# Score tiles and groups of transposes in pairs in the attention heads of an encoder trunk

## The chip, the cores and the metric

The kernel runs on one core of a Trainium2 chip. The core has a matrix engine (TensorE, PE in the profile; its weight loads have a row of their own, PEld), three engines for elementwise work (VectorE or DVE, ScalarE or ACT, GpSimd or POOL), and DMA queues, most of them issued from SyncE (SP). PE reads its operands from on-chip memory and writes into PSUM, from where ACT and DVE fetch the results. The metric is the device time of one execution in microseconds. Three runs of the kernel before gave 1676.1, 1676.44 and 1677.04; the median is 1676.44.

## The reference

Two sequences of 512 tokens and 1024 features go through a trunk of two layers: a Fourier mixing layer and an attention layer, each followed by an MLP with a squared ReLU. Only the attention matters here. It has 8 query heads of 128 features that share 2 key and value heads; queries and keys are normalised and rotated first.

```python
def one_block(q_blk):
    s = jnp.einsum("bqkgd,bskd->bkgqs", q_blk, k)
    p = jax.nn.softmax(s, axis=-1)
    return jnp.einsum("bkgqs,bskd->bqkgd", p.astype(v.dtype), v)
```

So for each of 2 x 8 pairs of sequence and head, a 512 x 512 matrix of scores is made from queries and keys, each row becomes a softmax, and the result weighs the values.

## The kernel before

Operands of matmuls are split into a high and a low half of a reduced 32-bit format, and a product of two split operands is made of three matmuls (high by high, high by low, low by high) that accumulate in one PSUM tile: `mm3`, lines L81 to L83. A split is a cast on ACT (L86) and a subtraction on DVE (L87). Elsewhere in the kernel the same product is written as `product` (L927). PSUM holds eight tiles of 128 x 512.

The work on one head has these parts:

- `transpose_q` (L1497): four 128 x 128 transposes turn the query of a head into one PSUM tile, which is split.
- `scores` (L1508 to L1512), once for each of four tiles of 128 queries: three matmuls; the row maximum, negated, on DVE (L1508); the exponential with the row's sum on ACT (L1510); the reciprocal of the sum on DVE (L1511); the normalisation on POOL (L1512). Each tile of probabilities takes one of eight buffers of a pool of temporaries.
- `transpose_p` (L1518), once for each of four tiles of 128 keys: four transposes, one out of each of the head's four probability tiles, fill one PSUM tile, which is split. So the first group already needs all four tiles of the head.
- `values`: twelve matmuls over the four transposed tiles; the result is copied out of PSUM on ACT (L1534), and for the first sequence it is split too.

The loop over the heads is staggered: in turn n it makes the scores of head n and transposes the probabilities of head n - 1, then the query of head n + 1 is transposed, then the values of head n - 1 are multiplied. Turns 1 to 15 have both scores and transposes; the last turn, 16, has transposes and values only. The scores of the first head stand before the loop.

```python
for n in range(1, len(heads) + 1):
    pts, nxt = [], []
    for t in range(NT):
        if n < len(heads):
            nxt.append(scores(*heads[n], qT, t))
        k, both = transpose_p(probs, t)
        pts.append(k)
        ...
    if n + 1 < len(heads):
        qT = transpose_q(*heads[n + 1])
    values(*heads[n - 1], pts)
```

Two further jobs are threaded through the loop. From the third turn, a piece of deferred normalisation and rotation of queries (`todo`, on ACT, DVE and POOL) follows the first group of transposes. From the seventh turn, weights of the output projection are loaded ahead over SP, and in each of eight turns one of them is split (`fresh`; L86 and L87 with the operand w); that split is placed behind the split of the turn's last transposed tile and behind the last exponential and reciprocal.

What sets the order: in blocks marked `manual_schedule` the engines named there keep the written order. The loop over heads stands in no such block, so a planner orders every engine's instructions by its own estimates, with the written order as preference. The projection behind the loop (from L1740) again has PE's order written out.

Of the kernel before, what the change touches and what calls it, by code (L numbers as in the profile page):

```python
# [44 lines left out]
def trunk_kernel(ctx, tc, x_in, xt_in, y_out, tables, rope, gfour, gcol, grow, gfin,  # L45
# [22 lines left out]
    def tm(shape=(P, 512), dt=F32):  # L68
        return tmp.tile(list(shape), dt, tag="t2", name=nm("t"))

    def small(n=4):
        return sm.tile([P, n], F32, tag="s", name=nm("s"), padded_shape=[P, 8])

    def ps():
        return psp.tile([P, 512], F32, tag="ps", name=nm("ps"))
# [4 lines left out]
    def mm3(out, lh, ll, rh, rl, first, last):  # L80
        nc.tensor.matmul(out, lh, rh, start=first, stop=False)  # L81
        nc.tensor.matmul(out, lh, rl, start=False, stop=False)  # L82
        nc.tensor.matmul(out, ll, rh, start=False, stop=last)  # L83
# [5 lines left out]
    def behind(x, y, sync=False):  # L89

        kind = mybir.DependencyClass.Sync if sync else mybir.DependencyClass.NoSync
        tc.add_manual_dep(x.ins, y.ins.name, mybir.DependencyInfo(kind, mybir.DependencyReason.SCHED_ONLY),
                          reason="order")
# [1338 lines left out]
    def head_squares(raw, h0, n, ss, scale=1.0):  # L1432
        junk = tm((P, n * HD), BF16)
        for h in range(h0, h0 + n):
            nc.scalar.activation(junk[:, (h - h0) * HD : (h - h0 + 1) * HD], raw[:, h * HD : (h + 1) * HD],
                                 AF.Square, scale=scale, accum_out=ss[:, h : h + 1])
# [56 lines left out]
    def transpose_q(q, h):  # L1493
        pt = ps()
        c = (h % 2) * HD
        for t in range(NT):
            nc.tensor.transpose(pt[:, t * P : (t + 1) * P], qr[q, h // 2][:, t, c : c + HD], ident)  # L1497
        qT = slot([P, 2, 512], F32R)
        split(qT[:, 0], qT[:, 1], pt)
        return qT  # L1500

    def scores(q, h, qT, t):
        kk = kT[q, h // 4]
        s = ps()
        cols = slice(t * P, (t + 1) * P)
        mm3(s, qT[:, 0, cols], qT[:, 1, cols], kk[:, 0], kk[:, 1], True, True)
        m, sm_ = small(1), small(1)
        nc.vector.tensor_reduce(m[:, :1], s, AX.X, ALU.max, negate=True)  # L1508
        p = tm()
        last_made[:] = [nc.scalar.activation(p, s, AF.Exp, bias=m[:, :1], accum_out=sm_[:, :1]),  # L1510
                        nc.vector.reciprocal(sm_[:, :1], sm_[:, :1])]  # L1511
        nc.gpsimd.tensor_scalar(p, p, sm_[:, :1], 1.0, ALU.mult, ALU.mult)  # L1512
        return p

    def transpose_p(probs, sc):
        pt = ps()
        for t in range(NT):
            nc.tensor.transpose(pt[:, t * P : (t + 1) * P], probs[t][:, sc * P : (sc + 1) * P], ident)  # L1518
        k = slot([P, 2, 512], F32R)
        return k, split(k[:, 0], k[:, 1], pt)  # L1520

    def values(q, h, pts):
        o = ps()
        c = (h // 4) * HD
        for sc in range(NT):
            vh, vl = vt[q][0][:, sc, c : c + HD], vt[q][1][:, sc, c : c + HD]
            mm3(o, vh, vl, pts[sc][:, 0], pts[sc][:, 1], sc == 0, sc == NT - 1)
        i, j = h // 2, h % 2
        name = "b11" if h < 4 else "b21"
        if j == 0:  # L1530
            heads_out.f[q, i] = slot([P, 2, 512], F32)
            if q == 0:
                heads_out.b.setdefault(name, []).append([slot([P, 2, 512], F32R) for _ in range(2)])
        nc.scalar.copy(heads_out.f[q, i][:, j], o)  # L1534
        if q == 0:
            hi, lo = heads_out.b[name][-1]
            split(hi[:, j], lo[:, j], o)
# [143 lines left out]
    heads = [(q, h) for q in range(NSEQ) for h in range(NH)]  # L1681
    raw, ss = slot([P, 1024], F32), small(8)
    with tc.manual_schedule(engines={ET.Activation}):
# [4 lines left out]
        qT = transpose_q(*heads[1])  # L1688
# [9 lines left out]
    for n in range(1, len(heads) + 1):  # L1698
        pts, nxt = [], []
        for t in range(NT):  # L1700
            if n < len(heads):
                nxt.append(scores(*heads[n], qT, t))
            k, both = transpose_p(probs, t)
            pts.append(k)
            if t == NT - 1 and fresh:
                for a, b, c in zip(fresh.pop(), both, last_made):
                    behind(a, b)
                    if nxt:
                        behind(a, c)
            if n > 2 and t == 0:  # L1710
                for _ in range(3 if n == 3 else 1):
                    next(todo, None)
        last = nxt[-1] if nxt else last
# [3 lines that stand above are left out]
        if n == 2:  # L1717
            head_squares(raw, 4, 4, ss)
        probs = nxt
        if n > 6:  # L1720
            next(first_rows, None)
# [373 lines left out]
```

## Time and profile before

The profiled execution took 1677.68 us, of which the span from the first to the last instruction is 1675.9 us.

| | |
|---|---|
| median of three runs | 1676.44 us |
| profiled execution; its span | 1677.68 us; 1675.9 us |
| PE busy | 1662.2 us (99%) |
| PEld, DVE, ACT, POOL busy | 1386.9, 1265.2, 870.0, 391.0 us |
| mean granted clock of PE | 0.999 |
| loop over heads, first transposes to the projection | 844.56 to 965.65 us |

How to read it: the busy time of an engine is a share of the whole span and says nothing of a single stage. The row of a stretch gives the same numbers for that stretch alone. The chain of work that ended last is followed back from the last instruction; a millisecond of PE in it means that PE waited for nothing in that time. A row of the timeline gives start, length, engine, line, operation, output and inputs, and in brackets the idle time before it with what ended it. Rows of consecutive instructions of one kind are merged (x4), and as matmuls are pipelined their lengths overlap: the distance between starts is what one of them costs.

### The profile page before, as it was taken

To read this page: it belongs to the slowest core of one execution; us is meant where nothing else is said; L and a number is where in the kernel's file an instruction comes from. 1 tells how busy PE (TensorE), PEld (TensorE's weight loads), DVE (VectorE), ACT (ScalarE), POOL (GpSimd) and SP (SyncE) were. 2 spreads that over 40 slices of the span, in tenths; PEclk is the share of its full clock that TensorE was granted. 3 is DMA by queue.
4 is the path that set the end of the run, shared out by engine and by line. 5 is a ranking of instruction groups with operands and counts; after the bars stand their busy time and mean duration, and the time that the engine had idled before them with its cause. 6 is when DMAs were issued, how large, how long until landed. Compare 5 with 4: busy or idle time off the path is not lost.

```text
span 1675.9 us, 22279 instructions
## 1 busy us (share of the span) xinstructions
PE 1662.2 (99%) x7845; PEld 1386.9 (83%) x7845; DVE 1265.2 (75%) x1847; ACT 870.0 (52%) x1536; POOL 391.0 (23%) x364
## 2 busy tenths in 40 slices
PE   9999999999999999999999999999999999999998
PEld 8988888888888888888888888888888888888887
DVE  8779786557886869869888877777855487978865
ACT  6766444446343435446688854554454552433334
POOL 3321443221000001324454302004422220000002
PEclk9999999999999999999999999999999999999999
DMA  9843655449775757525501155334544696757522
GB/s 309 255 160 107 210 182 188 156 163 371 257 226 164 246 172 236 177 69 191 172 1 39 63 178 212 126 119 168 210 145 166 219 381 191 230 157 246 168 101 101
DMA packets 122048, 303.00 MB, mean 181 GB/s; under 512 B 12200, under 2 KB 13352, under 8 KB 121936
## 3 DMA queue, kind: packets, MB, share of 16 engines
q1 hardware_dynamic: 98576, 254.05, 43.6%
q0 software_dynamic: 8960, 21.05, 5.9%
q10 hardware_dynamic: 14400, 26.48, 4.2%
q8 instruction: 61, 1.00, 0.2%
q14 instruction: 51, 0.42, 0.1%
HBM read 218.11 MB, written 82.38 MB: 179 GB/s over the span
## 4 chain that ended last, share of the span: by engine, by line
PE 95%; DVE 2%; DMA 1%; ACT 1%; issue 1%; POOL 0%; SPq 0%; DVEq 0%; POOLq 0%; ACTq 0%
PE ps L927 73%; PE ps L83 6%; PE ps L81 6%; PE ps L82 6%; PE ps L1518 2%; DMA u<-x 0%; DMA u<-w_four 0%; PE ps L1497 0%; DVE w L87 0%; PE ps L191 0%; DMA raw<-w_up 0%; PE ps L496 0%; PE ps L493 0%; DVE u L238 0%; DVE raw L975 0%
## 5 line engine op out<-in xcount | busy, mean ns | idle before, releaser
L927 PE MATMUL ps<-u,w 128*128 128x512 f32 x4944 | 1131.1, 389 | 1.3 <-DVE u L1730 1.3
L927 PEld LDWEIGHTS ps<-u,w 128*128 128x128 f32 x4944 | 926.5, 188 | 196.3 <-ACT u L958 1.9
L86 ACT CAST w<-raw 128x1024 fp32r<-128x1024 f32 (+1 forms) x216 | 213.8, 994 | 311.8 <-PE ps L927 233.8
L87 DVE TENSOR_TENSOR w<-raw,w 128x1024 fp32r<-128x1024 f32 (+1 forms) x216 | 252.4, 1172 | 76.3 <-ACT w L86 76.1
L86 ACT CAST u<-u 128x1024 fp32r<-128x1024 f32 x144 | 145.0, 1047 | 84.1 <-PE ps L927 38.3
L87 DVE TENSOR_TENSOR u<-u,u 128x1024 fp32r<-128x1024 f32 x144 | 173.8, 1233 | 17.0 <-ACT u L86 15.7
L927 PE MATMUL ps<-u,u 128*128 128x512 f32 x600 | 143.1, 389 | 0.5 <-DVE t L1012 0.5
L1133 DVE TENSOR_TENSOR u<-ps,u 128x512 f32<-128x512 f32 x160 | 109.4, 685 | 39.2 <-PE ps L927 37.0
L1160 POOL DMA_DIRECT2D raw<-w_sum x32 | 27.7, 865 | 469.3 <-DMA raw<-w_sum 195.6
L1043 POOL TENSOR_TENSOR u<-u 128x512 f32<-128x512 f32 x28 | 37.6, 1344 | 426.0 <-ACT u L940 426.0
L927 PEld LDWEIGHTS ps<-u,u 128*128 128x128 f32 x600 | 112.4, 188 | 24.5 <-DVE t L1012 0.9
L81 PE MATMUL ps<-u,u 128*128 128x512 f32 (+2 forms) x340 | 128.7, 380 | 0.0
L83 PE MATMUL ps<-u,u 128*128 128x512 f32 (+2 forms) x340 | 124.0, 366 | 0.0
L82 PE MATMUL ps<-u,u 128*128 128x512 f32 (+2 forms) x340 | 123.6, 365 | 0.0
L182 POOL TENSOR_TENSOR t<-t,t 128x512 f32<-128x512 f32 (+1 forms) x54 | 77.6, 1442 | 186.7 <-ACT t L178 185.8
L939 ACT ACTIVATE t<-t 128x512 f32<-128x512 f32 x64 | 40.5, 632 | 110.0 <-DVE t L1012 96.5
L83 PEld LDWEIGHTS ps<-u,u 128*128 128x128 f32 x340 | 64.2, 189 | 10.8 <-DVE u L87 0.3
L87 DVE TENSOR_TENSOR u<-ps,u 128x512 fp32r<-128x512 f32 (+3 forms) x112 | 68.1, 634 | 5.6 <-ACT u L86 5.1
L82 PEld LDWEIGHTS ps<-u,u 128*128 128x128 f32 x340 | 64.4, 189 | 8.4 <-DVE u L87 0.3
L81 PEld LDWEIGHTS ps<-u,u 128*128 128x128 f32 x340 | 64.4, 189 | 7.8
L999 DVE TENSOR_TENSOR t<-ps,u 128x512 f32<-128x512 f32 x32 | 22.0, 687 | 59.7 <-PE ps L927 56.0
L86 ACT CAST u<-ps 128x512 fp32r<-128x512 f32 (+3 forms) x112 | 59.4, 556 | 7.6 <-PE ps L1518 6.1
(265 smaller groups left out, 2015.3 us busy)
## 6 DMA issues: line engine op xcount, KB each, us to landing
raw<-w_up SPq DMA_DIRECT2D x80, 512.0 KB, 4.6
u<-spill_t SPq DMA_DIRECT2D x60, 512.0 KB, 6.9
raw<-w_sum SPq DMA_DIRECT2D x56, 512.0 KB, 5.6
u<-spill_b SPq DMA_DIRECT2D x45, 512.0 KB, 6.4
spill_t<-u SPq DMA_DIRECT2D x84, 256.0 KB, 2.0
spill_b<-t ACTq DMA_DIRECT2D x60, 256.0 KB, 4.3
raw<-w_row SPq DMA_DIRECT2D x28, 512.0 KB, 5.1
park<-u SPq DMA_DIRECT2D x24, 512.0 KB, 4.5
```

The lines of the kernel that those rows point to most:

```text
L81: nc.tensor.matmul(out, lh, rh, start=first, stop=False)
L82: nc.tensor.matmul(out, lh, rl, start=False, stop=False)
L83: nc.tensor.matmul(out, ll, rh, start=False, stop=last)
L86: hi = nc.scalar.copy(dst_hi, src)
L87: return hi, eng.tensor_sub(dst_lo, src, f32(dst_hi))
L182: nc.gpsimd.tensor_add(acc[q][:, :n], acc[q][:, :n], s[:, :n])
L927: nc.tensor.matmul(o, w[x][:, sl], h[k][y], start=first and k + i == 0, stop=k == n - 1 and i == 2, skip_group_check=not first)
L939: nc.scalar.activation(t, src, AF.Relu)
L1043: eng.tensor_sub(t[:, 0], b12, b11)
L1133: return nc.vector.tensor_add(x, o, x)
L1160: nc.gpsimd.dma_start(s[:, 1], w[:, 3], accum_op=ALU.add)
L1518: nc.tensor.transpose(pt[:, t * P : (t + 1) * P], probs[t][:, sc * P : (sc + 1) * P], ident)
```

## The change

Two score tiles are made in one go, at the even tiles, where one was made at each tile. The groups of transposes stay where they are in the loop, so that two score tiles are followed by two groups of transposes, twice per head. No instruction is added or taken away, and no operand changes.

```diff
     for n in range(1, len(heads) + 1):
         pts, nxt = [], []
         for t in range(NT):
-            if n < len(heads):
-                nxt.append(scores(*heads[n], qT, t))
+            if n < len(heads) and t % 2 == 0:
+                nxt += [scores(*heads[n], qT, i) for i in range(t, t + 2)]
             k, both = transpose_p(probs, t)
             pts.append(k)
             if t == NT - 1 and fresh:
```

## The prediction

> **What bounds the kernel now.** I read the page first: busy time by engine, then the chain that ended last.
>
> ```profile
> span 1675.9 us, 22279 instructions
> ...
> PE 1662.2 (99%) x7845; PEld 1386.9 (83%) x7845; DVE 1265.2 (75%) x1847; ACT 870.0 (52%) x1536; POOL 391.0 (23%) x364
> ...
> PE 95%; DVE 2%; DMA 1%; ACT 1%; issue 1%; POOL 0%; SPq 0%; DVEq 0%; POOLq 0%; ACTq 0%
> ```
>
> TensorE (PE) is busy for all but 13.7 us of the span and carries 95% of the chain. So I narrow the views to the loop over heads, which is all that the change touches. The table by stretch gives it one row, and the waits of that stretch name who held up PE's weight loads (PEld), which run just ahead of its matmuls.
>
> ```profile
> 844.56:965.65 121.09, 120.84 (x683) 100.45 (x682) 106.65 (x227) 105.12 (x258) 49.07 (x70) 1.00 0.11 36
> ```
>
> ```profile
> PEld ps L1518 <- POOL t L1512: 1.3, 4, 0.6
> PEld ps L82 <- DVE u L87: 0.3, 2, 0.2
> PEld ps L83 <- DVE u L87: 0.3, 1, 0.3
> ```
>
> The columns of the first are length, then busy time of PE, PEld, DVE, ACT and POOL, granted clock, DMA share, GB/s. The stage is 121.09 us long, 7.2% of the span; PE is busy for 120.84 of them at full clock, while VectorE (DVE, 106.65) and ScalarE (ACT, 105.12) follow close. The only waits of weight loads come to 1.9 us, and 1.3 of them are for the probabilities that POOL normalises (L1512) and the transposes (L1518) read. A reordering on PE can win here what is lost to waits or to switching between kinds of work; it can lose whatever it makes late on DVE and ACT.
>
> **The change, part by part.** It adds and removes no instruction. In each of 15 heads (n = 1 to 15) the order s0 T0 s1 T1 s2 T2 s3 T3 becomes s0 s1 T0 T1 s2 s3 T2 T3 (s: a score tile of three matmuls, L81 to L83; T: a group of four transposes, L1518). So 30 times a score tile moves ahead of one group of transposes, and its maximum (DVE), exponential (ACT), reciprocal (DVE) and normalisation (POOL) move with it ahead of that group's cast (ACT) and subtraction (DVE). Behind T3 stand, as before, the transposes of the next query (Q, L1497) and the twelve matmuls of the values. No DMA moves against another; the deferred rotary step that follows the first T of a head (n > 2) now stands behind two score tiles.
>
> Switching on PE. The chain in order of time, from the fourth head on, prices each kind in both neighbourhoods:
>
> ```profile
> 861.11 0.23 PE ps L83
> 861.35 0.44 PE ps L1518 x4
> 861.78 0.23 PE ps L81
> ...
> 863.39 0.23 PE ps L83
> 863.62 0.44 PE ps L1518 x4
> 864.06 0.44 PE ps L1497 x4
> 864.49 0.23 PE ps L81
> ```
>
> A group of four transposes between matmuls takes 0.44 us (861.35 to 861.78), and so does each of two groups in a row (863.62 to 864.49 is 0.87); a matmul takes 0.23 us before and behind a group. So merging groups saves 0.87 to 0.88 against 0.87: between 0 and 0.01 us per merge, 2 merges per head, 15 heads, 0 to 0.3 us. A coarser reading gives a wider upper end, from the starts of one undisturbed head (timeline of PE):
>
> ```profile
> 946.18 0.60 PE L1518 MATMUL ps<-ident,t 128*128 128x128 f32 x4
> ...
> 949.60 0.60 PE L1518 MATMUL ps<-ident,t 128*128 128x128 f32 x4
> ...
> 950.39 0.48 PE L81 MATMUL ps<-u,u 128*128 128x512 f32 x1
> 950.70 0.40 PE L82 MATMUL ps<-u,u 128*128 128x512 f32 x1
> ...
> 952.79 0.39 PE L82 MATMUL ps<-u,u 128*128 128x512 f32 x1
> ...
> 953.47 0.39 PE L82 MATMUL ps<-u,u 128*128 128x512 f32 x1
> ...
> 953.93 0.60 PE L1518 MATMUL ps<-ident,t 128*128 128x128 f32 x4
> 960.55 2.21 PE L1518 MATMUL ps<-ident,t 128*128 128x128 f32 x16
> 962.52 0.47 PE L81 MATMUL ps<-u,u 128*128 128x512 f32 x1
> ```
>
> From 950.70 to 953.93 are 14 matmuls: 0.231 each. Three turns of s and T take 3.42 (946.18 to 949.60), so a lone group is 1.14 - 0.692 = 0.448; the eight transposes with the matmul behind them take 1.10 (949.60 to 950.70), so two groups together are 0.869. That is 0.027 per merge, 0.8 us in all. I take 0.2, nearest to the chain, whose rows are ends and not starts; the ends are 0 and 0.8.
>
> Waits that go. The undisturbed head lasts 953.93 - 946.18 = 7.75 us. Heads with rotary work in them last longer:
>
> ```profile
> 860.05 0.60 PE L1518 MATMUL ps<-ident,t 128*128 128x128 f32 x4
> ...
> 868.09 0.38 PE L1518 MATMUL ps<-ident,t 128*128 128x128 f32 x2
> ...
> 876.10 0.49 PE L1518 MATMUL ps<-ident,t 128*128 128x128 f32 x3
> ...
> 907.51 0.60 PE L1518 MATMUL ps<-ident,t 128*128 128x128 f32 x4
> ```
>
> 860.05 to 876.10 is two heads, 16.05 against 15.50: 0.55 lost. 876.10 to 907.51 is four heads, 31.41 against 31.00: 0.41 lost. The last sixteen transposes take 1.97 us (960.55 to 962.52) against 16 x 0.11 = 1.76: 0.2 lost. All that can be won back is 1.2 us. What these wait for is close to late even in the undisturbed head (POOL's and DVE's timeline; the fourth probability tile is the one on POOL):
>
> ```profile
> 952.89 0.70 POOL L1512 TENSOR_SCALAR t<-t,s 128x512 f32<-128x512 f32 x1 [0.56 <-DVE s L1511]
> ```
>
> ```profile
> 950.11 0.69 DVE L87 TENSOR_TENSOR u<-ps,u 128x512 fp32r<-128x512 f32 x1
> 950.72 0.68 DVE L1508 TENSOR_REDUCE s<-ps 128x1 f32<-128x512 f32 x1
> 951.32 0.15 DVE L1511 RECIPROCAL s<-s 128x1 f32<-128x1 f32 x1
> 951.39 1.27 DVE L87 TENSOR_TENSOR u<-ps,u 128x512 fp32r<-128x512 f32 x2
> 952.57 0.15 DVE L1511 RECIPROCAL s<-s 128x1 f32<-128x1 f32 x1
> 953.04 1.08 DVE L87 TENSOR_TENSOR w<-u,w 128x512 fp32r<-128x512 f32 x1 [0.32 <-ACT w L86]
> ```
>
> The tile is ready at 953.59 and first read at 953.93: 0.34 us to spare. After the change two score tiles instead of one lie between the values and T0, which makes T0 3 x 0.23 = 0.69 us later, and s3 ends one group, 0.44 us, earlier. So up to 1.1 us is added to those 0.34, and waits for POOL should mostly go. Since the same engines serve a burst now, I book half of the 1.2: 0.6 us; ends 0 and 1.2.
>
> What is late next. DVE spaces maxima and subtractions by 0.60 (950.72 to 951.32) and reciprocals by 0.07. From the end of s2 to the second matmul of the next head's s0, which reads the low half of Q, PE will need s3 0.69, T2, T3 and Q 1.31, values 2.77 and one matmul 0.23: 5.0 us. In it DVE has two maxima, three subtractions and two reciprocals, 3.14 us, and the subtraction of T1 if that is left over, 0.60: 1.2 us to spare. Before, Q's subtraction ended at 951.39 + 1.27 = 952.66 and was read at 953.47, 0.8 to spare; T3's low half, done by about 952.05, was read at 952.79, 0.7 to spare. So the cover is not thinner than now, unless DVE takes the split of a kept weight (L87, w<-u,w, 1.08 us, one in each of eight heads) in between. I book 0.2 us for stray waits of that sort; ends 0 and the slow rival's price below. PSUM: a head takes ten of the pool's tiles, eight stand in the pool, so a buffer comes round after eight tenths of 7.75, 6.2 us. The fourth score tile, begun three matmuls before 949.60, so at 948.9, is held until its exponential, which ends before the reciprocal at 952.57: 3.7 us; a burst that puts two more places of 0.60 in front of it still leaves 1.3 us. I book nothing; without that cover it would be the same 0.60 per head as the slow rival's.
>
> The sum, on the profiled execution (1677.68 us, of which 1675.9 is span): 1677.68 - 0.2 - 0.6 + 0.2 = 1677.1. That execution lies 1.24 above the median of the runs, 1676.44, so against the median the forecast is 1675.8. Its own range is 1674.4 (0.8 + 1.2 won) to 1676.8 (nothing won, 0.4 of strays).
>
> **The rivals.** No change at all (0.12): no block with a written order stands around the loop, so the planner may fall back to single turns where it thinks a tile not ready; the same page of waits would remain and the time would be 1676.4. For it: at 868.09 it already split a group of transposes. Against: the plain head follows the written order exactly.
>
> Switching costs more than I read (0.08). Behind a group the first matmul occupies 950.39 to 950.70, 0.31 instead of 0.23. If the 0.08 were lost time and not the end of the last transpose, 30 merges would give 2.4, and with all waits gone 1676.44 - 2.4 - 1.2 = 1672.8, 0.2% faster. Against it speaks the chain, where the matmul behind a group takes 0.23.
>
> Slower (0.18): the burst of s2, s3, T2, T3, Q makes DVE late in the eight heads with a weight split. The split is due behind T3's subtraction and the fourth reciprocal; now it stands behind Q's subtraction too (953.04 comes last). If in the burst it slips ahead of Q's subtraction, 1.2 us to spare becomes 0.1, and ACT's share of the chain, a cast and an exponential, is not yet in that. If it costs one DVE place, 0.60, in eight heads, the loss is 4.8 less the 0.6 of waits won: 1676.44 + 4.2 = 1680.6. It decides from about 0.5 us per head in eight heads (4.0 less 0.6 is 3.4). Against it: PE can take T0 or s1 of the next head meanwhile, as the planner's own swaps show, and DVE has 14.4 us of idle time in the stage.
>
> The clock falls (0.01). The longest run of transposes grows from eight to twelve, 1.3 us. If those ran at half clock, 12 x 0.11 x 15 = 20 us would be added: 1696. Against it: sixteen transposes ran within 960.55 to 962.52, and the stage's granted clock reads 1.00. The Trainium skill ("TensorE: Matmul & The Clock Gate", Part 4: PE-mode transpose) says that transposes do not count as activity for the clock as matmuls do, which speaks for this rival; by that rule longer runs of transposes could let the clock fall, and the trace shows no such fall even in a longer run.
>
> The stage behind moves (0.03): a loop that ends earlier or later changes what the transfers for the next stage collide with; nothing here prices that, and I put it at 2 us to either side, since PE's order there is written out.
>
> **How the numbers follow.** Forecast 0.58, the others as given. About 0.2%, 3.4 us, is what a measurement of this kernel can tell from no change: faster means below 1673.1, slower above 1679.8. Faster: half of the switching rival, 0.04. Slower: somewhat over half of the slow rival, 0.10, and the clock, 0.01: 0.11. The rest, 0.85, is the same. The range 1673.0 to 1680.0 takes in the forecast, no change, the mild half of the switching rival and the mild part of the slow one; it leaves out about 0.04 + 0.08 + 0.01.
>
> **What would show it.** Right: PE's timeline shows six matmuls, then eight transposes, then six matmuls, then twelve transposes; two groups in a row take 0.87; the undisturbed head stays within 0.06 of 7.75; the waits of L1518 for L1512 fall below 1.3; 876.10 to 907.51's counterpart shortens towards 31.0. Wrong: waits of L82 or L83 for L87 grow beyond 1 us, above all in the later heads; the head falls below 7.65; or the time moves outside the stage.

## The result, and the profile after

The kernel with pairs takes 1679.55 us (median of 19 runs) against 1676.52 for the kernel before (19 runs): the ratio is 1.0017, 95% interval 1.0011 to 1.0024, so 3.0 us slower. Forecast was 1675.8, 0.6 us faster. The time lies within the range that was given, but on the wrong side of the kernel before.

The page of the kernel with pairs:

```profile
span 1678.0 us, 22288 instructions
...
PE 1664.5 (99%) x7845; PEld 1387.3 (83%) x7845; DVE 1267.0 (76%) x1847; ACT 870.0 (52%) x1536; POOL 392.2 (23%) x364
...
PE 92%; DVE 4%; ACT 1%; DMA 1%; issue 1%; POOL 0%; SPq 0%; DVEq 0%; ACTq 0%; POOLq 0%
```

PE is still busy 99% of the span, but its share of the chain has fallen from 95% to 92% and that of DVE has risen from 2% to 4%. The loss lies in the loop over heads alone. To measure that stage in both traces I take the first matmul on a weight of the last projection before the loop (PE's timeline) and the first copy behind it (L1750, whose row gives first and last start), and for what follows the first transpose of the output (L1864). First the kernel before, then the one with pairs; in each, one row of the timeline and two rows of the views by line:

```profile
838.29 0.49 PE L81 MATMUL ps<-w,u 128*128 128x512 f32 x1
```

```profile
L1750 ACT COPY t<-ps x4: 582/589/589, 968.4 to 982.0; 128x512 f32<-128x512 f32 x4
```

```profile
L1864 PE MATMUL ps<-ident,u x16: 270/272/273, 1641.0 to 1642.7; 128*128 128x128 f32 x16
```

```profile
837.29 0.49 PE L81 MATMUL ps<-w,u 128*128 128x512 f32 x1
```

```profile
L1750 ACT COPY t<-ps x4: 589/589/589, 970.9 to 984.5; 128x512 f32<-128x512 f32 x4
```

```profile
L1864 PE MATMUL ps<-ident,u x16: 270/272/273, 1643.5 to 1645.2; 128*128 128x128 f32 x16
```

The stage takes 968.4 - 838.3 = 130.1 us before and 970.9 - 837.3 = 133.6 with pairs, 3.5 more. From there to the output it is 672.6 in both. So nothing came from the stages behind. The span grew by only 2.1 us, because the profile with pairs reaches the stage 1.0 us earlier and is 0.4 us shorter behind the first transpose of the output.

The waits of weight loads from 844.5 to 970 us, with pairs:

```profile
PEld ps L82 <- DVE u L87: 5.1, 15, 0.6
PEld ps L81 <- ACT u L86: 1.5, 5, 0.4
PEld ps L83 <- DVE u L87: 1.4, 2, 0.7
PEld ps L1518 <- POOL t L1512: 0.4, 1, 0.4
```

The waits for POOL's probabilities fell from 1.3 to 0.4 us, as forecast. In their place stand 8.0 us of waits for splits (L86, L87), where there were 0.6; not all of it is lost time, since a weight load runs ahead of its matmul. Of the 5.1 us in the first row, 3.8 lie between 863 and 902 us, in stretches 3 to 7 of the table below; the second products of the values (L82), which read the low halves of the transposed tiles, wait there. The 1.4 us of L83 are two waits for the low half of a query, both behind 916 us.

Where this falls is seen turn by turn. The table gives the time from one start of a query's transposes (L1497 in PE's timeline) to the next, so "3" is the stretch from Q in turn 3 to Q in turn 4. Stretches 4 to 7 hold one group of the deferred rotary products each, stretch 3 the first steps of that work; weight splits fall into the stretches from 9 on. The clear stretches are 2 and 8, and 9, where the split stands behind Q's subtraction before and after (914.54 and 914.82 in DVE's timelines) and costs 0.02 us at most.

| kernel | 1, 2 | 3 | 4 to 7 (rotary) | 8, 9 | 10 to 13 (weight splits) | 1 to 13 |
|---|---|---|---|---|---|---|
| before | 7.76 7.72 | 8.32 | 7.76 7.90 7.87 7.89 | 7.72 7.74 | 7.74 7.73 7.74 7.73 | 101.6 |
| pairs | 7.74 7.71 | 8.48 | 8.17 8.14 8.17 8.11 | 7.71 7.71 | 8.46 7.89 8.02 8.53 | 104.8 |

Clear stretches (2, 8, 9) became shorter by 0.01 to 0.03. The rotary stretches lost 0.22 to 0.41 each, 1.2 us in all; stretches 10 to 13 lost 2.0 us; stretch 3 lost 0.16. Two different things happen there.

*Weight splits.* DVE's timeline of stretch 10 with pairs, then POOL's, then PE's:

```profile
920.44 1.29 DVE L87 TENSOR_TENSOR u<-ps,u 128x512 fp32r<-128x512 f32 x2
921.64 0.15 DVE L1511 RECIPROCAL s<-s 128x1 f32<-128x1 f32 x1
922.12 1.08 DVE L87 TENSOR_TENSOR w<-u,w 128x512 fp32r<-128x512 f32 x1 [0.32 <-ACT w L86]
923.12 0.68 DVE L87 TENSOR_TENSOR u<-ps,u 128x512 fp32r<-128x512 f32 x1
```

```profile
921.96 0.70 POOL L1512 TENSOR_SCALAR t<-t,s 128x512 f32<-128x512 f32 x1 [0.72 <-DVE s L1511]
```

```profile
922.96 0.39 PE L82 MATMUL ps<-u,u 128*128 128x512 f32 x1
923.19 0.40 PE L81 MATMUL ps<-u,u 128*128 128x512 f32 x1
923.85 0.50 PE L83 MATMUL ps<-u,u 128*128 128x512 f32 x1 [0.27 <-DVE u L87]
```

The weight's subtraction now runs ahead of the subtraction that makes Q's low half (923.12); in the rows of before it came last, behind Q's. PE has begun two score tiles of the next head and stops, since the third product needs that half. On ACT the weight's cast runs ahead of Q's as well:

```profile
921.45 0.64 ACT L86 CAST w<-u 128x512 fp32r<-128x512 f32 x1
921.96 0.61 ACT L86 CAST u<-ps 128x512 fp32r<-128x512 f32 x1
```

The split stands ahead of Q's subtraction in stretches 10, 11 and 13. In 10 and 13 POOL's normalisation began first, the split takes 1.08 us, and these stretches lose 0.72 and 0.80; in 11 DVE began first, the split takes 0.69 (930.52), and the loss is 0.16. In stretch 12 it stands behind Q's subtraction (939.14), and there the planner chose another order of casts and subtractions for the turn, which loses 0.28.

*Rotary products.* One such step, two products on DVE (L1474) and one on POOL (L1471); before, then with pairs:

```profile
869.67 0.48 DVE L1474 TENSOR_TENSOR t<-u,u 128x128 f32<-128x128 f32 x2
```

```profile
869.01 0.74 POOL L1471 TENSOR_TENSOR t<-u,u 128x256 f32<-128x256 f32 x1
```

```profile
870.42 1.02 DVE L1474 TENSOR_TENSOR t<-u,u 128x128 f32<-128x128 f32 x2
871.37 0.68 DVE L87 TENSOR_TENSOR u<-ps,u 128x512 fp32r<-128x512 f32 x1
```

```profile
870.53 0.77 POOL L1471 TENSOR_TENSOR t<-u,u 128x256 f32<-128x256 f32 x1
```

Before, POOL had all but finished when DVE began. With pairs both begin within 0.11 us, and DVE's two products take 1.02 us in place of 0.48. The subtractions of the transposed tiles stand behind them, and the values wait for what these make: with pairs, in each of the four stretches, one second product of the values (L82) starts 0.46 us behind the first and the third 0.34 behind that, where 0.23 is usual.

### The profile page after: what moved, and what is told of

Same layout as the page of the kernel before. It is cut to its first block, busy times and chain, and to the rows that moved or that the text cites. A ratio compares the mean times of both kernels' runs of the same rounds, so it can differ in the third digit from the quotient of the medians.

```text
span 1678.0 us, 22288 instructions
## 1 busy us (share of the span) xinstructions
PE 1664.5 (99%) x7845; PEld 1387.3 (83%) x7845; DVE 1267.0 (76%) x1847; ACT 870.0 (52%) x1536; POOL 392.2 (23%) x364
## 4 chain that ended last, share of the span: by engine, by line
PE 92%; DVE 4%; ACT 1%; DMA 1%; issue 1%; POOL 0%; SPq 0%; DVEq 0%; ACTq 0%; POOLq 0%
PE ps L927 73%; PE ps L83 5%; PE ps L82 5%; PE ps L81 5%; PE ps L1518 1%; DVE u L87 1%; DVE s L1508 1%; DMA u<-x 0%; DVE w L87 0%; DMA u<-w_four 0%; ACT t L1510 0%; PE ps L191 0%; PE ps L496 0%; DMA raw<-w_up 0%; PE ps L493 0%
## 5 line engine op out<-in xcount | busy, mean ns | idle before, releaser
L86 ACT CAST w<-raw 128x1024 fp32r<-128x1024 f32 (+1 forms) x216 | 213.6, 994 | 310.5 <-PE ps L927 243.9
L87 DVE TENSOR_TENSOR w<-raw,w 128x1024 fp32r<-128x1024 f32 (+1 forms) x216 | 252.5, 1172 | 75.8 <-ACT w L86 75.6
L86 ACT CAST u<-u 128x1024 fp32r<-128x1024 f32 x144 | 145.1, 1047 | 81.4 <-PE ps L927 36.8
L87 DVE TENSOR_TENSOR u<-u,u 128x1024 fp32r<-128x1024 f32 x144 | 173.4, 1231 | 17.5 <-ACT u L86 16.4
L81 PE MATMUL ps<-u,u 128*128 128x512 f32 (+2 forms) x340 | 126.5, 375 | 0.0
L82 PE MATMUL ps<-u,u 128*128 128x512 f32 (+2 forms) x340 | 125.0, 368 | 0.4
L83 PE MATMUL ps<-u,u 128*128 128x512 f32 (+2 forms) x340 | 124.0, 366 | 0.5 <-DVE u L87 0.5
L82 PEld LDWEIGHTS ps<-u,u 128*128 128x128 f32 x340 | 64.3, 189 | 13.6 <-DVE u L87 5.1
L83 PEld LDWEIGHTS ps<-u,u 128*128 128x128 f32 x340 | 64.1, 189 | 11.4 <-DVE u L87 1.4
L81 PEld LDWEIGHTS ps<-u,u 128*128 128x128 f32 x340 | 64.2, 189 | 10.3 <-ACT u L86 1.5
L87 DVE TENSOR_TENSOR u<-ps,u 128x512 fp32r<-128x512 f32 (+3 forms) x112 | 68.4, 634 | 5.4 <-ACT u L86 4.7
L1512 POOL TENSOR_SCALAR t<-t,s 128x512 f32<-128x512 f32 x64 | 47.2, 738 | 74.9 <-DVE s L1511 49.7
```

The costliest lines, as they stand in the source:

```text
L86: hi = nc.scalar.copy(dst_hi, src)
L87: return hi, eng.tensor_sub(dst_lo, src, f32(dst_hi))
```

## The experiments

Theory W: the weight split ahead of Q's subtraction is one part of the loss. Theory R: the rotary products that run beside POOL's are the other. Theory B, the rival: the burst as such, two score tiles and two groups, makes DVE late in any turn.

Each kernel below was run 11 times (the last 5 times) beside the kernel before. The intervals are some 0.09%, 1.4 us, to either side, so the whole time of a kernel can hardly tell a single loss from none. The stretches can: the pairs alone and the second kernel below have the same order on every engine, and in the stretches that its edit does not touch their profiles agree within 0.03 us. The expectations of the first two kernels count turns from one first group of transposes to the next, so their numbers differ a little from the stretches here.

**The weight split behind Q.** The weight's cast and subtraction are put behind Q's as an order told to the planner; nothing else is edited.

```diff
-        split(qT[:, 0], qT[:, 1], pt)
+        q_made[:] = split(qT[:, 0], qT[:, 1], pt)
...
-                for a, b, c in zip(fresh.pop(), both, last_made):
+                for a, b, c in zip((weight := fresh.pop()), both, last_made):
...
             qT = transpose_q(*heads[n + 1])
+            [behind(a, b) for a, b in zip(weight, q_made)]
```

> Pairs kept; in the turns with a weight split, that split is put behind Q's cast and subtraction. In the profile of the pairs it ran ahead of Q's subtraction in some turns, at 922.12 and at 946.55 for 1.08 us each, and these two turns lasted 8.48 and 8.54 against 7.71. Theory W (the weight split delays the query of the next head): the turns from 916.17 to 956.98 come back to about 7.71, which gives back up to 2.3 us of their excess; the time falls from 1679.6 to 1677.3 to 1678. Theory R (the rotary step on DVE and POOL is the cause): the two long turns may shrink, but the time falls by less than 0.7, since the loss lies in the turns before. Theory B (the burst of two score tiles and two groups makes DVE late in every turn): no change beyond 0.5 us.

It takes 1678.2 us against 1676.8 of the kernel before in the same set, ratio 1.0008 (1.0000 to 1.0017): 1.4 us above it, where the pairs alone are 3.0 above. Stretches 10 to 12 are 7.71, 7.76 and 7.73; the rotary stretches stay at 8.13 to 8.18. Stretch 13 stays at 8.08: at 944.25 a product of the values starts 0.45 us behind the one before it. With the next edit added it is 7.72, although the order on every engine is the same in both kernels, so what is left there is not a matter of order; its cause stays open. Q's subtraction and the weight's, in that order, in DVE's timeline of this kernel:

```profile
945.15 0.69 DVE L87 TENSOR_TENSOR u<-ps,u 128x512 fp32r<-128x512 f32 x1 [0.28 <-ACT u L86]
945.76 0.68 DVE L87 TENSOR_TENSOR w<-u,w 128x512 fp32r<-128x512 f32 x1
```

In the stretches this is W, and not B. The planner's other orders change along with it: the products of two score tiles that were interleaved on PE in stretches 10, 11 and 13 stand in plain order again, and so do the casts and subtractions of turn 12.

**The rotary products apart.** POOL's product is told to wait for DVE's two.

```diff
-            eng.tensor_mul(t1, x, every(table[:, 0, t]))
+            first = eng.tensor_mul(t1, x, every(table[:, 0, t])) if eng is nc.vector else None
             ...
-                nc.vector.tensor_mul(t2[:, :, sl], x[:, :, other], every(table[:, 1, t, sl]))
+                made = nc.vector.tensor_mul(t2[:, :, sl], x[:, :, other], every(table[:, 1, t, sl]))
+            first or behind(eng.tensor_mul(t1, x, every(table[:, 0, t])), made, True)
```

> Pairs kept; POOL's product of the rotary step waits until DVE's two products of that step are done, so that the two engines no longer read and write on-chip memory for it at the same time. Order on every engine unchanged. In the profile of the pairs the two DVE products took 1.02 to 1.11 us where POOL's ran beside them, before 0.47 to 0.48. Theory R: the products fall back to about 0.5, the four turns from 868.16 to 900.76, which last 8.11 to 8.18, come to about 7.75, and the time falls by 1.3 to 1.8, to about 1678. Theory W: these turns get no shorter than by 0.1 each and the time stays at 1679.6. Theory B: no change either.

1678.18 us, ratio 1.0005 (0.9996 to 1.0014): again 1.4 above the kernel before. The rotary stretches fall to 7.71, 7.72, 7.75 and 7.73, while 10 to 13 keep 8.47, 7.86, 8.04 and 8.53. DVE's products (now L1473) and POOL's (now L1474):

```profile
870.37 0.48 DVE L1473 TENSOR_TENSOR t<-u,u 128x128 f32<-128x128 f32 x2
```

```profile
871.02 0.73 POOL L1474 TENSOR_TENSOR t<-u,u 128x256 f32<-128x256 f32 x1 [0.53 <-PE ps L1518]
```

All four engines run the same instructions in the same order as with pairs alone; only POOL's product starts later. So the 0.5 to 0.7 us that DVE lost per step, and the 0.4 us that each of these stretches won back, are the price of running side by side, and R holds.

**Both edits, with pairs and with single turns.** The same two edits, once on the pairs and once on the kernel before.

> Pairs kept, with both edits: the weight split behind Q's subtraction, and POOL's rotary product behind DVE's. Theories W and R together: the gains add, 1679.6 - 2.0 - 1.5 = about 1676, level with the kernel before or up to 0.8 us faster, since merged groups of transposes cost a little less. Theory B: 1679 or more.

> Single score tiles and groups as in the kernel before, with the same two edits as in the run with both. It tells whether pairs win or lose once both covers are restored. If pairs cost nothing in themselves, this is level with the kernel before, 1676.0 to 1676.5, and not faster than the pairs with both edits. If pairs lose by themselves (theory B), it is 1676 and the pairs with both edits are 1 us or more slower.

Pairs with both take 1676.55 (0.9996, 0.9987 to 1.0005), single turns with both 1676.46 (0.9997, 0.9988 to 1.0006): both level with the kernel before, and with each other. The two gains add up: 3.0 - 1.4 and 3.0 - 1.4 give 1.6 each, 3.2 together, and pairs with both stand 3.3 better than pairs alone, which is clear of the intervals. Taken by stretches, pairs with both need 101.2 us for 1 to 13, single turns 101.6, as before. So the pairs' own gain is some 0.4 us, too little for these runs to show in the whole time. Most of it lies in the rotary stretches, which take 7.73 to 7.76 with pairs and 7.73 to 7.90 with single turns.

**Half of the change.** First the first two score tiles alone in a pair, then the last two alone.

```diff
-            if n < len(heads) and t % 2 == 0:
-                nxt += [scores(*heads[n], qT, i) for i in range(t, t + 2)]
+            if n < len(heads) and t != 1:
+                nxt += [scores(*heads[n], qT, i) for i in range(t, max(t + 1, 2))]
```

```diff
+            if n < len(heads) and t != 3:
+                nxt += [scores(*heads[n], qT, i) for i in range(t, t + 1 + t // 2)]
```

> Half of the change: only the first two score tiles of a turn stand together (s0 s1 T0 T1 s2 T2 s3 T3). In DVE's order of this kernel the weight split stays behind Q's subtraction, as in the kernel before, while the rotary products move as with both pairs. Theory W + R: the long turns with a weight split (8.46, 7.89, 8.02, 8.53) go, the rotary turns stay at about 8.1, so 1679.6 - 1.4 = about 1678.2. If what costs is each swap of a score tile with a group, half of the 3 us goes: 1678.1 as well, but then spread over all turns and not in those two groups.

> The other half: only the last two score tiles stand together (s0 T0 s1 T1 s2 s3 T2 T3). In DVE's order the weight split runs ahead of Q's subtraction as with both pairs, and the rotary step keeps its place from the kernel before. Theory W + R: the rotary turns are at most 7.9 as before, and the turns with a weight split stay long, so again about 1678.2, with the loss in the late turns only.

The first pair alone takes 1677.8 (1.0008, 0.9999 to 1.0017), the last alone 1679.02 (1.0014, 1.0005 to 1.0022). The places are as expected: with the first pair the loss lies in stretches 5 to 7 (8.35, 8.36, 8.44) and stretches 10 to 13 are 7.71 to 7.72; with the last pair the rotary stretches are 7.71 to 7.92 and 10 to 13 are 8.34, 8.28, 8.28, 8.66. The sizes are not: stretches 10 to 13 lose 2.6 us with the last pair alone and 2.0 with both, and the whole 2.1 instead of 1.4; the first pair alone loses 0.9 in the whole (the interval reaches no change) and 1.4 by stretches. In its stretch 4 POOL's product began 0.44 us ahead of DVE's, which took 0.66, and the stretch is 7.80. DVE's rotary products under the first pair, then under the last:

```profile
878.22 1.17 DVE L1474 TENSOR_TENSOR t<-u,u 128x128 f32<-128x128 f32 x2
886.57 1.24 DVE L1474 TENSOR_TENSOR t<-u,u 128x128 f32<-128x128 f32 x2
```

```profile
877.34 0.47 DVE L1474 TENSOR_TENSOR t<-u,u 128x128 f32<-128x128 f32 x2
892.91 0.47 DVE L1474 TENSOR_TENSOR t<-u,u 128x128 f32<-128x128 f32 x2
```

So each half of the change brings one of the two losses: the first pair the meeting of the rotary products, the last pair the weight split's step ahead of Q.

**The first rotary steps spread.** What is left with both edits is stretch 3, 8.47 us, with three steps at once. One per turn:

```diff
-                for _ in range(3 if n == 3 else 1):
+                for _ in range(1):
```

> Pairs with both edits of before (weight split behind Q's subtraction, POOL's rotary product behind DVE's), and the three first steps of the deferred rotary work taken one per turn instead of three in turn 3, so that all of it comes two turns later. With both edits the turn after the third Q still lasts 8.47 against 7.71; if that is the three steps on ACT and DVE, it falls to about 7.75 and the time by 0.7, to 1675.9, 0.5 to 0.9 below the kernel before. Rival: the steps cost the same wherever they stand, or the later turns with a weight split take the loss over, and it stays at 1676.5.

> Single score tiles and groups with the same three edits. It tells whether pairs add anything once the covers are whole. From the turns: with pairs a clear turn lasts 7.71, single ones 7.74, and single turns with rotary work 7.88 against 7.73; so this should fall less than the pairs, to about 1676.0. If it falls as far as the pairs, pairing is worth nothing.

Pairs take 1675.93 (0.9994, 0.9985 to 1.0003), single turns 1676.52 (1.0000, 0.9991 to 1.0008). Stretch 3 falls to 7.72 with pairs, but stretch 5, which now holds the four small operations L157 to L160 (one on ACT, three on DVE, not four on DVE), is 8.05; 1 to 13 take 100.8. With single turns stretches 5 and 9 are 8.26 and 8.28, and 1 to 13 take 101.9; the 1676.0 that was expected of them did not come. The pairs are the fastest kernel of the study by their median, 0.9 us below the kernel before, but the interval reaches over no change.

A further spread, two of those four operations per turn, was run to see whether that stretch can go too:

```diff
-        for f in steps[2:]:
-            f()
+        for i, f in enumerate(steps[2:]):
+            f(); (yield) if eng is nc.gpsimd and i == 1 else None
```

> Pairs with both edits and the first rotary steps spread further: the four small operations on DVE that still made one turn 8.05 long come in two turns, two each. If that turn is long because of them, it falls to 7.75 or so and the kernel to 1675.6, about 1 us below the kernel before. Rival: the step only moves, into the turns with a weight split, and it stays at 1675.9 or more.

1676.75 (0.9997, 0.9988 to 1.0006). Stretch 5 becomes 7.70, but stretch 7 is 8.19, and 9 and 10 are 7.86 and 7.95: the work only moved, into turns with other extra work. The expectation of 1675.6 was wrong and its rival right.

**The change doubled.** All four score tiles, then all four groups, with both edits.

```diff
+            if n < len(heads) and t == 0:
+                nxt += [scores(*heads[n], qT, i) for i in range(NT)]
```

> The change doubled: all four score tiles of a turn, then all four groups of transposes (s0 s1 s2 s3 T0 T1 T2 T3), with the two edits (weight split behind Q's subtraction, POOL's rotary product behind DVE's). A clear turn holds one more merge of groups than with pairs; by 7.74 for single and 7.71 for pairs it should last 7.69. Theory W + R: with both covers restored the longer burst costs nothing more, and the time is 1676.3 to 1676.6. Theory B, the burst as such makes DVE late: values wait for the low halves of T2 and T3 in every turn, 0.3 to 0.6 each, and the time is 1680 to 1685.

1685.95 (1.0054, 1.0040 to 1.0067), a little beyond the range of theory B; the 1676.3 to 1676.6 of W + R did not come. Here theory B holds, in every turn: stretches 10 to 13 last 8.18 to 8.27, the others 8.32 to 8.91. The waits of weight loads in the stage and the row of one of them in PE's timeline:

```profile
PEld ps L82 <- DVE u L87: 12.4, 25, 0.5
```

```profile
925.89 0.50 PE L82 MATMUL ps<-u,u 128*128 128x512 f32 x1 [0.21 <-DVE u L87]
```

DVE's and ACT's timelines of the next turn show why: the tiles' casts and subtractions come in one block behind the last exponential, while the values already run.

```profile
932.91 0.16 DVE L1511 RECIPROCAL s<-s 128x1 f32<-128x1 f32 x1
933.38 2.48 DVE L87 TENSOR_TENSOR u<-ps,u 128x512 fp32r<-128x512 f32 x4 [0.32 <-ACT u L86]
```

```profile
932.08 0.71 ACT L1510 ACTIVATE t<-ps,s 128x512 f32<-128x512 f32 x1
932.75 2.06 ACT L86 CAST u<-ps 128x512 fp32r<-128x512 f32 x4
```

So a burst does run out of cover, but somewhere above two score tiles and by four; three were not run.

## Why the prediction was wrong

- *Switching on PE*: right. Four rows of PE's timeline with pairs:

```profile
903.89 0.60 PE L1497 MATMUL ps<-ident,u 128*128 128x128 f32 x4
911.60 0.60 PE L1497 MATMUL ps<-ident,u 128*128 128x128 f32 x4
919.31 0.60 PE L1497 MATMUL ps<-ident,u 128*128 128x128 f32 x4
927.77 0.60 PE L1497 MATMUL ps<-ident,u 128*128 128x128 f32 x4
```

  A clear turn is 7.71 against 7.72 to 7.74, so about 0.02 per turn, between the 0.01 of the forecast (0.2 in 15 turns) and its upper end of 0.05. That is the upper end of the chain's reading, 0 to 0.01 per merge; the coarser reading, 0.027 per merge, was too high.
- *Waits that go*: right for POOL's probabilities (1.3 to 0.4 us), wrong in what it was to bring. I booked 0.6 us of the excess of the rotary turns as won; they lost 1.2 instead, since what ends last there with pairs is DVE, not POOL. With POOL's product behind DVE's the gain is there: these four stretches then take 0.4 to 0.5 us less than in the kernel before, while single turns with the same edits gain nothing in them. So the term was sound and was covered by the loss below.
- *What is late next*: this is the step that failed, booked at 0.2 us and measured at about 3.3 by stretches (1.2 in the rotary turns, 2.0 in 10 to 13, 0.16 in turn 3). Its list of DVE's work between s2 and the next score tile left out the rotary products altogether, and the change moved those to stand beside POOL's. I had written that the rotary step "now stands behind two score tiles" and not asked what runs on POOL at that time. The weight split stood in the list, but as an exception with a chance, not as a cost. One reading in it was off to the safe side: Q's low half is read by the third matmul of s0 (L83, the wait at 923.85), not the second, so there was 0.23 us more to spare than was worked out.
- *The slow rival* named the right mechanism for the larger part: the weight split slipping ahead of Q's subtraction. It was priced at 0.60 in eight heads, 4.8 us; it cost 0.72, 0.16, 0.28 and 0.80 in four stretches, 2.0 us. Against it I had set that PE could take other work meanwhile and that DVE has 14.4 us of idle time in the stage. PE did take products of a second score tile (923.19) and still stopped, and idle time elsewhere in the stage did not help. The split was tied only to T3's subtraction and the last reciprocal; nothing tied it to Q's, and that an order not written down may change with any other edit was the sentence missing there. How much of the 2.0 us is the place of the split, and how much the longer subtraction beside POOL's normalisation in stretches 10 and 13, no run separates.
- *No change at all*: excluded. The planner followed the pairs, and the time moved beyond its interval.
- *The switching rival* and *the clock*: excluded by clear turns of 7.71 and by the granted clock, 0.999 in both profiles. With four groups and Q in a row, 20 transposes (the doubled change), it also read 0.999.
- *PSUM and the stage behind*: right as far as the traces go; a wait for a buffer would stand at the first matmul of a tile, L81 or a transpose, and in the list above those wait for a cast (L86) or for POOL, neither of which is the last to read a buffer; and the stages behind took 672.6 us in both.

## What to carry to other kernels

A reordering on an engine that is 99% busy won little by itself here, 0.4 of 1676 us by the stretches, but it re-dealt the order of the other engines, which a planner arranges. What it re-deals has to be walked through turn by turn, turns with extra work first. Tie down every order on which the bound depends, rather than one that happens to hold. And where two engines share work on on-chip memory, ask not only how long each operation takes but what runs beside it.

## What the runs showed of the hardware

DVE and POOL delay each other when DVE reads both its operands from SBUF, the on-chip memory beside PSUM, while POOL reads from it too. DVE's pair of 128 x 128 products takes 0.47 to 0.48 us alone and 1.02 to 1.24 where it began 0.1 to 0.3 us ahead of POOL's product. Taken singly, DVE's eight products in the stage with pairs last 281 to 820 ns, where a product alone takes some 280: POOL's product gets in between the two, and the second is the long one. The weight's subtraction takes 0.68 alone (945.76 above) and 1.08 beside POOL's normalisation (922.12). The other side pays as well, as DVE's and POOL's timelines of stretch 11 with pairs show:

```profile
930.52 0.69 DVE L87 TENSOR_TENSOR w<-u,w 128x512 fp32r<-128x512 f32 x1
```

```profile
930.57 1.21 POOL L1512 TENSOR_SCALAR t<-t,s 128x512 f32<-128x512 f32 x1 [0.56 <-DVE s L1511]
```

Here DVE began 0.05 us earlier and kept its 0.69, and POOL took 1.21 in place of 0.70; where POOL began first, at 921.96, DVE took the longer time. Subtractions with one operand in PSUM took 0.66 to 0.69 throughout, also beside POOL's work. The Trainium skill ("SBUF — State Buffer", Who interferes with whom) states this rule: a DVE instruction with two inputs in SBUF contends with a GpSimd instruction that reads SBUF, one with at most one SBUF input does not (outside DVE's two-port modes), and the one issued first goes first. The rows agree on the first two points. On the third they agree where DVE began first and where POOL began 0.07 us or more ahead; where POOL began less than 0.05 us ahead, as in stretch 9 with pairs (POOL at 914.78, DVE at 914.82), DVE kept its 0.69 and POOL took 1.21, so starts that close do not tell which was issued first. The 1.08 us of the weight split in the trace of before was already such a meeting, and the stretches with it took 7.73 or 7.74 there, as long as the clear ones.
